# Full-height low queries, an early second normalisation and 14 instead of 12 block products in a hybrid attention block

## The chip, the cores and the metric

The kernel runs on one core of a Trainium2 chip. The core has TensorE (PE; its weight loads are shown apart as PEld), VectorE (DVE), ScalarE (ACT), GpSimd (POOL) and SyncE (SP), which here issues the DMA transfers. Each engine works through its own list of instructions in order. The metric is the time of one execution in microseconds (us), as the median of several runs.

## The reference

One layer on x of 2048 tokens by 1024 columns, float32:

```python
xn = rms_norm(x, norm_gain)
proj = xn @ w_in       # qa ka va ga | qb kb vb gb | iq ik iw | za zb
# branch A: 8 heads of 64, chunks of 64 tokens, own chunk + 8 before, relative bias
ya = chunked_relpos_attention(qa, ka, va, rel_bias) * silu(ga)
# branch B: indexer -> the 256 best keys of each query -> attention on these, one kb/vb for 8 heads
score = sum_h relu(iq_h @ ik.T) * iw_h;  idx = top_k(score, 256)
yb = softmax(qb @ kb[idx].T) @ vb[idx] * silu(gb)
merged = sigmoid(za + b0) * (ya @ w_branch_a) + sigmoid(zb + b1) * (yb @ w_branch_b)
out = rms_norm(x + merged @ w_out, final_norm_gain)
```

## The kernel before, in words

Numbers are kept as pairs: a float32 value is split into a high part (a rounded copy) and a low part (what is left), and a product of two values is three matmuls, high by high, high by low, low by high (`mm3`, L214). A split is a copy by ScalarE and a subtraction by VectorE or GpSimd. Scores of branch A hold both parts of a key's 64 dims on the 128 rows of `kk`; the query's high part stands on both halves (`m = 0`), and its low part on 64 rows alone (`m = 1`), so each score tile is one matmul over 128 rows and one over 64 (L899).

The stages, with their place in the profiled execution:

- To about 119 us: x is loaded and normalised, and the indexer's columns and kb are made.
- 119 to 774 us: the projection. Tokens stand in four groups of 512, and two groups fit into SBUF at a time (slots 0 and 1 of `xh`, `xl`). The columns form 20 units of 256. The list `jobs` first takes all units for groups 0 and 1, then va and some "rest" units for groups 3 and 2. Between them these groups are loaded and normalised into the slots again (`norm_again`, `split_x`: one VectorE instruction scales by gain and root, L226, ScalarE copies, L227, VectorE subtracts, L228); GpSimd makes sums of the blocks on the way (L1214 to L1217), and what others need later goes through scratch memory (`xnD`, `sumD`).
- Beside it runs the search for the 256 best keys: TensorE makes logits (L476), ScalarE takes their positive part (L478), VectorE adds them up (L483) and then brackets a threshold for each query (L511 to L566). `pump` writes search steps into the program while a budget lasts: after each pair of chains `tick` grants `PUMP`, or `PUMP2` in the rest units, times a factor. At the end a check (L574 to L578) asks whether any query has missed its count; TensorE takes part in it with one matmul.
- About 800 to 1050 us: 12 "quads". For groups 3 and 2 a unit is made as a product of two-by-two blocks with 7 products of 12 matmuls in place of 8 (84 for 96); `QUADS` names the units, `prep_full` makes the combinations of weights, `first` and `rest_of` the products.
- About 1050 to 1925 us: the attention. `a_unit` (4 groups by 8 heads, L899 scores, L903 exponentials, L933 transposes, L943 values) and `b_unit` (L1008, L1011, L1025, L1033) interleave by a cost table, with the products with the branch weights (`branch`) between them. A score tile goes from TensorE to VectorE (bias, running minimum, L830), to ScalarE (exponential), back to TensorE (transpose), to ScalarE with VectorE or GpSimd (split, L846 to L854), and to TensorE again.
- To the end: the product with w_out and the last normalisation.

The order on each engine is set by a scheduler that models the time of each instruction as the program is written; `prep`, `tick` and the place in `jobs` decide where something can stand. SP issues nearly all transfers, in its order.

Of the kernel before, what the change touches and what calls it, by code (L numbers as in the profile page):

```python
# [8 lines left out]
F32 = mybir.dt.float32  # L9
# [30 lines left out]
BLOCKS = [2, 4, 5, 6, 7, 8, 9, 10, 11, 12, 13, 14, 15, 3]  # L40
PUMP, PUMP2 = 4500, 6900
SQD = (2,)
# [9 lines left out]
WE = False  # L52
QUADS = "za ka za gb za ka gb qb ga qa ga qa"
WSB, NB = 4, 5
# [25 lines left out]
def f32(ap):  # L80
    return ap.bitcast(F32)
# [11 lines left out]
def block_kernel(ctx: ExitStack, tc: tile.TileContext, io, dbg=None):  # L93
# [11 lines left out]
    def scratch(name, shape, dt=F32):  # L105
        if dbg is not None and name in dbg:
            return nc.dram_tensor("dbg_" + name, shape, dt, kind="ExternalOutput").ap()
        return dram.tile(shape, dt, name=name)
# [14 lines left out]
    sBD = [scratch(f"sBD{g}", [D, 512]) for g in range(NG)]  # L123
    xnD = scratch("xnD", [4, 128, 2, 512])
    sumD = scratch("sumD", [4, 4, 128, 512])
# [622 lines left out]
    mid_st = ExitStack()  # L748
    bres = {}

# [18 lines left out]
    def load_sum(n, k):  # L769

        if n == "s3":
            hi, lo = A21(k)
        else:
            hi, lo = (t[:, k] for t in sums_[n])
        nc.sync.dma_start(f32(lo), sumD[("s3", "s1", "s2", "s4").index(n), k])
        nc.scalar.activation(hi, f32(lo), AF.Copy)
        nc.vector.tensor_tensor(lo, f32(lo), f32(hi), op=OP.subtract)  # L777

# [77 lines left out]
    def load_a(G, h):  # L856
        base = max(0, 4 * G - 4)
        q = ld.tile([128, 2, 512], F32R, name="qs", tag="qs")
        for hl, half in ((0, 0), (0, 1), (1, 0)):
            nc.sync.dma_start(f32(q[half * 64:half * 64 + 64, hl, :]), qA[G][hl, :, h, :])  # L860
        kk = ld.tile([128, 1024], F32R, name="kk", tag="kk")
        v = ld.tile([128, 8, 128], F32R, name="vs", tag="vs")
        for i, g in enumerate(range(max(0, G - 1), G + 1)):
            nc.sync.dma_start(f32(kk[:, i * 512:i * 512 + 512]), kA[g].rearrange("l r h n -> (l r) h n")[:, h, :])
            nc.sync.dma_start(f32(v[:, 4 * i:4 * i + 4]), vA[g][h])
        return base, q, kk, v

    def a_unit(G, h):
        st = {}

        def loads():
            if "ld" not in st:
                st["ld"] = load_a(G, h)
            if h % 2 == 0 and wz is not None:
                sg = wz.tile([128, 512], F32, name="sg", tag="sg", bufs=SGB)
                nc.sync.dma_start(sg, gAD[G][(h // 2) * 128:(h // 2) * 128 + 128])
                shared["sg", "a", h // 2] = sg

        def one():
# [8 lines left out]
            for j in range(4):  # L888
# [6 lines left out]
                for a, w, add in segs:  # L895
                    s_ps = next_s()
                    ko = (f - base) * 128 + a
                    for m, r in ((0, 128), (1, 64)):
                        nc.tensor.matmul(s_ps[:, :w], q[:r, m, j * 128:(j + 1) * 128], kk[:r, ko:ko + w],  # L899
                                         start=(m == 0), stop=(m == 1))  # L900
                    softmax_piece(s_ps[:, :w], add, a == 0, P[:, j, a:a + w], mx[:, j:j + 1])
                    yield
# [286 lines left out]

    rate = [PUMP]  # L1190

    def tick(x):
        if threads:
            pump(rate[0] * x)
        elif not early_:
            close_search()

    again = []

    def norm_again(g):  # L1200

        def part(k):
            xs = tkl.tile([128, 2, 512], F32, name="xs", tag="xs", bufs=2)
            nc.sync.dma_start(xs, io["xT"][g][:, k::4, :])
            if g == 2:
                xa = tkl.tile([128, 2, 512], F32, name="xa", tag="xa", bufs=1)
                nc.sync.dma_start(xa, xnD[k])
            for z in range(2):
                split_x(SLOT[g], k + 4 * z, xs[:, z], roots[g])
            if g == 3:  # L1210
                nc.sync.dma_start(xnD[k], xs)
                return
            e = nc.gpsimd
            e.tensor_tensor(xa[:, 1], xa[:, 1], xa[:, 0], op=OP.add)  # L1214
            e.tensor_tensor(xa[:, 0], xs[:, 0], xa[:, 0], op=OP.subtract)
            e.tensor_tensor(xs[:, 0], xa[:, 1], xs[:, 0], op=OP.subtract)
            e.tensor_tensor(xs[:, 1], xs[:, 1], xs[:, 0], op=OP.subtract)  # L1217
            for t, n in ((xa, 0), (xs, 2)):
                nc.sync.dma_start(sumD[n:n + 2, k].rearrange("s p n -> p s n"), t)

        return [lambda k=k: part(k) for k in range(4)]
# [40 lines left out]
    for i, (how, r_, u, g) in enumerate(jobs):  # L1262
        kind, c2 = UNITS[u]
        wt, s_ = wcur[r_], SLOT[g]
        if r_ >= nu and kind != "va":
            rate[0] = PUMP2
        for c in range(4 if kind == "va" else 2):
            acc = next_acc(i)
            if kind == "va":
# [5 lines left out]
                if again and c % 2 == 0:  # L1275
                    again.pop(0)()
                tick(0.25 if busy else 0.5)
            else:
# [5 lines left out]
                for _ in range(1 if busy and len(again) < 3 else 2):  # L1284
                    if again:
                        again.pop(0)()
                tick(0.5 if busy else 1)
        if (u, g) in ((b_, 0), (b_, 1)) and r_ < nu:
# [216 lines left out]
```

## Time and profile before

| | |
|---|---|
| median of 3 runs | 2142.16 us (2142.09 to 2147.2) |
| profiled execution | 2150.47 us, span 2148.4 us, granted TensorE clock 0.986 |
| TensorE, its weight loads | 2083.8 us (97%), 1713.9 us (80%) |
| VectorE, ScalarE, GpSimd | 68%, 59%, 36% |
| DMA | 327.45 MB, mean 152 GB/s |

A row of a group names line, engine, operation, output and inputs, shape and count; then busy time in us and the mean of one in ns; then idle time of the engine just before them and what ended it. A row of a windows table gives a stretch in us and the busy time of each engine in it, with counts, the granted clock, the share of the DMA engines' time and GB/s. A row of waits names who waited for whom: us in total, times, longest. "128\*128" or "64\*128" ahead of a shape are the rows and columns of the stationary operand.

### The profile page before, as it was taken

To read this page: it belongs to the slowest core of one execution; us is meant where nothing else is said; L and a number is where in the kernel's file an instruction comes from. 1 tells how busy PE (TensorE), PEld (TensorE's weight loads), DVE (VectorE), ACT (ScalarE), POOL (GpSimd) and SP (SyncE) were. 2 spreads that over 40 slices of the span, in tenths; PEclk is the share of its full clock that TensorE was granted. 3 is DMA by queue.
4 is the path that set the end of the run, shared out by engine and by line. 5 is a ranking of instruction groups with operands and counts; after the bars stand their busy time and mean duration, and the time that the engine had idled before them with its cause. 6 is when DMAs were issued, how large, how long until landed. Compare 5 with 4: busy or idle time off the path is not lost.

```text
span 2148.4 us, 33517 instructions
## 1 busy us (share of the span) xinstructions
PE 2083.8 (97%) x10730; PEld 1713.9 (80%) x10730; DVE 1450.5 (68%) x3712; ACT 1273.2 (59%) x2590; POOL 774.5 (36%) x931
## 2 busy tenths in 40 slices
PE   7799999999989999999899999999999999999998
PEld 7688888898878887877677888888878888887886
DVE  6758888869689737555456767756775677865444
ACT  5456675565655625554368768757876688873221
POOL 2131112222153127554235464445334543443420
PEclk9899999999999999999979999999999999999999
DMA  9473333444475325333656563455245531145642
GB/s 357 144 258 119 122 111 118 160 148 142 170 255 170 141 98 179 123 128 120 216 158 199 152 196 114 150 160 169 82 123 165 184 103 52 45 132 190 205 150 88
DMA packets 223044, 327.45 MB, mean 152 GB/s; under 512 B 28304, under 2 KB 99344, under 8 KB 222736
## 3 DMA queue, kind: packets, MB, share of 16 engines
q1 hardware_dynamic: 222864, 325.28, 47.2%
q8 instruction: 85, 1.39, 0.3%
q14 instruction: 95, 0.78, 0.1%
HBM read 215.13 MB, written 110.07 MB: 151 GB/s over the span
## 4 chain that ended last, share of the span: by engine, by line
PE 74%; DMA 11%; DVE 5%; POOL 4%; issue 3%; ACT 2%; SPq 1%; another core or an unknown queue 0%; DVEq 0%; POOLq 0%; ACTq 0%
PE acc L214 27%; PE d L214 8%; PE O L1033 6%; PE po L1400 6%; PE s L899 6%; PE s L1008 6%; PE pt L1025 6%; DMA wst<-wS 4%; PE O L943 4%; PE pt L933 3%; PE lg L476 3%; DMA mf<-mD 1%; POOL wst L1255 1%; DMA xrow<-x 1%; DMA wst<-wP 1%
## 5 line engine op out<-in xcount | busy, mean ns | idle before, releaser
L214 PE MATMUL acc<-xh,wt 128*128 128x512 f32 x1920 | 623.8, 395 | 5.4 <-DVE e L334 2.3
L214 PEld LDWEIGHTS acc<-xh,wt 128*128 128x128 f32 x1920 | 360.3, 188 | 91.6 <-ACT wt L1259 4.6
L214 PE MATMUL acc<-xl,wt 128*128 128x512 f32 x960 | 377.6, 393 | 0.1
L206 POOL TENSOR_TENSOR wt<-wst,wt 128x512 fp32r<-128x512 f32 (+1 forms) x116 | 150.7, 1329 | 471.9 <-ACT wt L205 443.3
L851 POOL TENSOR_TENSOR ptl<-pf,pth 128x512 fp32r<-128x512 f32 (+1 forms) x144 | 179.1, 1244 | 194.8 <-ACT pf L847 148.5
L854 DVE TENSOR_TENSOR ptl<-pt,pth 128x512 fp32r<-128x512 f32 (+1 forms) x288 | 187.3, 660 | 41.6 <-ACT pth L853 40.4
L214 PEld LDWEIGHTS acc<-xl,wt 128*128 128x128 f32 x960 | 181.0, 189 | 40.6 <-DVE xl L777 0.4
L478 ACT ACTIVATE lg<-lg 128x512 f32<-128x512 f32 (+2 forms) x304 | 152.4, 526 | 100.3 <-PE lg L476 97.9
L483 DVE SCALAR_TENSOR_TENSOR sc<-lg,iw,sc 128x512 f32<-128x512 f32 (+2 forms) x266 | 179.5, 679 | 42.0 <-ACT lg L478 37.2
L1008 PE MATMUL s<-kBt,qsB 128*128 128x512 f32 (+3 forms) x640 | 188.6, 386 | 1.1 <-DVE mx L830 0.8
L853 ACT ACTIVATE pth<-pt 128x512 fp32r<-128x512 f32 (+1 forms) x288 | 159.7, 577 | 41.2 <-PE pt L1025 19.2
L899 PE MATMUL s<-kk,qs 128*128 128x256 f32 (+2 forms) x464 | 165.4, 397 | 6.8 <-DVE mx L830 5.4
L1025 PE MATMUL pt<-ident,P 128*128 128x128 f32 x1088 | 165.9, 275 | 0.4 <-DVE ptl L854 0.2
L1011 ACT ACTIVATE P<-P,mx 128x128 f32<-128x128 f32 (+15 forms) x128 | 154.2, 1207 | 19.6 <-DVE mx L830 19.1
L1033 PE MATMUL O<-ptl,vBt 128*128 128x256 f32 x544 | 148.4, 300 | 1.0 <-POOL ptl L851 1.0
L1033 PE MATMUL O<-pth,vBt 128*128 128x256 f32 x544 | 148.0, 292 | 0.3
L830 DVE CUSTOM_DVE_ANT_0 P<-s,mk,mx 128x512 f32<-128x512 f32 (+2 forms) x192 | 125.2, 652 | 30.8 <-PE s L1008 25.3
L1025 PEld LDWEIGHTS pt<-ident,P 128*128 128x128 f32 x1088 | 125.6, 140 | 14.1 <-issue 2.6
L899 PEld LDWEIGHTS s<-kk,qs 128*128 128x128 f32 x464 | 90.2, 194 | 58.3 <-issue 33.0
L1071 POOL TENSOR_TENSOR dw<-dst,dw 128x512 fp32r<-128x512 f32 x64 | 82.6, 1291 | 133.8 <-ACT dw L1070 130.4
L214 PE MATMUL acc<-wt,xh 128*128 128x288 f32 x512 | 106.4, 302 | 12.8 <-DVE sm L547 4.7
L903 ACT ACTIVATE P<-P,mx 128x640 f32<-128x640 f32 (+4 forms) x128 | 97.6, 764 | 34.6 <-DVE mx L830 33.5
(286 smaller groups left out, 4599.5 us busy)
## 6 DMA issues: line engine op xcount, KB each, us to landing
wst<-wP SPq DMA_DIRECT2D x108, 256.0 KB
kk<-kA SPq DMA_DIRECT2D x56, 256.0 KB
vs<-vA SPq DMA_DIRECT2D x56, 256.0 KB
wst<-wS SPq DMA_DIRECT2D x48, 256.0 KB
qs<-qA SPq DMA_DIRECT2D x96, 128.0 KB
xrow<-x SPq DMA_DIRECT2D x16, 512.0 KB
sBD<-ef SPq DMA_DIRECT2D x32, 256.0 KB
vA<-eh SPq DMA_DIRECT2D x32, 256.0 KB
```

What stands on the lines that cost most here:

```text
L206: nc.gpsimd.tensor_tensor(wt[:, 1, k:k + n, c * 128:(c + 1) * 128], st, f32(hi), op=OP.subtract)
L214: nc.tensor.matmul(acc, a, b, start=(first and i == 0), stop=(last and i == n - 1), **({} if first and last else {"skip_group_check": True}))
L478: nc.scalar.activation(lg, lg, AF.Relu)
L483: nc.vector.scalar_tensor_tensor(o_, lg, wv, o_, op0=OP.mult, op1=OP.add)
L851: nc.gpsimd.tensor_tensor(lo, pf, f32(hi), op=OP.subtract)
L853: nc.scalar.activation(hi, src, AF.Copy)
L854: nc.vector.tensor_tensor(lo, src, f32(hi), op=OP.subtract)
L899: nc.tensor.matmul(s_ps[:, :w], q[:r, m, j * 128:(j + 1) * 128], kk[:r, ko:ko + w], start=(m == 0), stop=(m == 1))
L1008: nc.tensor.matmul(s_ps[:, :w], q[:, h, :], kBt[:, m, a:a + w], start=(m == 0), stop=(m == 1))
L1011: nc.scalar.activation(P[:, e, :n], P[:, e, :n], AF.Exp, bias=mx[:, e:e + 1], scale=-1.0, accum_out=st["sum"][:, (u % 2) * 2 + e:(u % 2) * ...
L1025: nc.tensor.transpose(pt[:, k, e, :], P[:, e, (kt + k) * 128:(kt + k + 1) * 128], ident)
L1033: nc.tensor.matmul(o_, vBt[:, kt + k, :], src[:, k, :], start=(kt + k == 0 and n_ == 0), stop=(kt + k == b and n_ == 1), skip_group_check= ...
```

## The change

1. `QUADS` names 14 units: two zb units go from the rest units (which then are 4) to the quads.
2. `norm_early` takes what `norm_again` did on a tile of its own: in jobs 6 to 20 the four parts of group 3 and of group 2 are loaded, scaled by ScalarE (gain) and multiplied by GpSimd (root), and written to scratch memory, each group to its own (`xnD2`, `xnD3`); the sums follow on GpSimd. `norm_again` now loads the finished values into the low half of the slot, and `split_in_place` makes the high half by a ScalarE copy and subtracts it in place on VectorE.
3. `load_a` uses two standing tiles for branch A's queries. Rows 64 to 128 of their low half are set to zero once by GpSimd; both matmuls of a score tile then run over 128 rows.
4. Budgets: `PUMP` is 5300 beside za, zb, ga, gb and 4500 beside qb, va, ka, qa; `PUMP2` 9000 in place of 6900; factors while a new group is being split are 0.35 and 0.75 in place of 0.25 and 0.5.

```diff
-PUMP, PUMP2 = 4500, 6900
+PUMP, PUMP2 = (5300, 4500), 9000
+DVE_KINDS = ("qb", "va", "ka", "qa")
+EN0, TQ = 6, 0.75
...
-QUADS = "za ka za gb za ka gb qb ga qa ga qa"
+QUADS = "za ka za gb za ka gb zb zb qb ga qa ga qa"
...
-    xnD = scratch("xnD", [4, 128, 2, 512])
+    xnD = {g: scratch(f"xnD{g}", [4, 128, 2, 512]) for g in (2, 3)}
...
-        q = ld.tile([128, 2, 512], F32R, name="qs", tag="qs")
+        if len(qz) < 2:
+            qz.append(ld.tile([128, 2, 512], F32R, name=f"qz{len(qz)}", tag="qs"))
+            nc.gpsimd.memset(f32(qz[-1][64:128, 1]), 0.0)
+        q = qz[rot("qz", 2)]
...
-                    for m, r in ((0, 128), (1, 64)):
-                        nc.tensor.matmul(s_ps[:, :w], q[:r, m, j * 128:(j + 1) * 128], kk[:r, ko:ko + w],
+                    for m in range(2):
+                        nc.tensor.matmul(s_ps[:, :w], q[:, m, j * 128:(j + 1) * 128], kk[:, ko:ko + w],
                                          start=(m == 0), stop=(m == 1))
...
+    def norm_early(g, k):
+
+        xs = tkl.tile([128, 2, 512], F32, name="xs", tag="xs", bufs=2)
+        nc.sync.dma_start(xs, io["xT"][g][:, k::4, :])
+        if g == 2:
+            xa = tkl.tile([128, 2, 512], F32, name="xa", tag="xa", bufs=1)
+            nc.sync.dma_start(xa, xnD[3][k])
+        e = nc.gpsimd
+        for z in range(2):
+            nc.scalar.activation(xs[:, z], xs[:, z], AF.Copy, scale=gcol[:, k + 4 * z:k + 4 * z + 1])
+            e.tensor_tensor(xs[:, z], xs[:, z], roots[g], op=OP.mult)
+        nc.sync.dma_start(xnD[g][k], xs)
+        if g == 3:
+            return
+        e.tensor_tensor(xa[:, 1], xa[:, 1], xa[:, 0], op=OP.add)
...
+    def split_in_place(hi, lo):
+
+        nc.scalar.activation(hi, f32(lo), AF.Copy)
+        nc.vector.tensor_tensor(lo, f32(lo), f32(hi), op=OP.subtract)
+
     def norm_again(g):
 
         def part(k):
-            xs = tkl.tile([128, 2, 512], F32, name="xs", tag="xs", bufs=2)
-            nc.sync.dma_start(xs, io["xT"][g][:, k::4, :])
...
             for z in range(2):
-                split_x(SLOT[g], k + 4 * z, xs[:, z], roots[g])
...
+                hi, lo = block(SLOT[g], z)(k)
+                nc.sync.dma_start(f32(lo), xnD[g][k][:, z])
+                split_in_place(hi, lo)
...
-        if r_ >= nu and kind != "va":
-            rate[0] = PUMP2
+        rate[0] = PUMP[kind in DVE_KINDS] if r_ < nu or kind == "va" else PUMP2
+        if EN0 <= i < EN0 + 16 and i % 2 == 0:
+            norm_early(3 - (i - EN0) // 8, (i - EN0) // 2 % 4)
...
-                tick(0.25 if busy else 0.5)
+                tick(0.35 if busy else 0.5)
...
-                tick(0.5 if busy else 1)
+                tick(TQ if busy else 1)
```

Three places show how the order moves. The first is VectorE's order where a group is made anew beside the search. `xs` holds loaded tokens, `xh`/`xl` the halves of a slot, `sc`/`lg` the search's scores and logits. Before:

```order
L483 SCALAR_TENSOR_TENSOR sc<-lg,iw,sc 128x384
L226 SCALAR_TENSOR_TENSOR xs<-xs,gcol,roots_135 128x512 x2
L483 SCALAR_TENSOR_TENSOR sc<-lg,iw,sc 128x384
L226 SCALAR_TENSOR_TENSOR xs<-xs,gcol,roots_135 128x512 x2
L228 TENSOR_TENSOR xl_122<-xs,xh_121 128x512
L483 SCALAR_TENSOR_TENSOR sc<-lg,iw,sc 128x384
L228 TENSOR_TENSOR xl_124<-xs,xh_123 128x512
```

and in the changed program, for the parts of group 2 in slot 0:

```order
L1230 TENSOR_TENSOR xl_119<-xl_119,xh_118 128x512
L568 TENSOR_SCALAR far<-sc 128x1792
L555 TENSOR_SCALAR jk,over<-sc,st 128x1920
L485 SCALAR_TENSOR_TENSOR sc<-lg,iw,sc 128x512 x2
L1230 TENSOR_TENSOR xl_119<-xl_119,xh_118 128x512
L711 SCALAR_TENSOR_TENSOR el<-acc,eh 128x512
L558 SCALAR_TENSOR_TENSOR sc<-jk,sc 128x1920
```

The scaling is gone from VectorE there; what is left is the subtraction, in place, between logits and search steps. The second place is GpSimd's order in the first half of the projection. `wt` are weights that it splits, `xa` the tile for the sums. Before:

```order
L1214 TENSOR_TENSOR xa<-xa 128x512
L206 TENSOR_TENSOR wt<-wst,wt 128x4x128 x44
L196 TENSOR_TENSOR wt<-wst,wt 128x8x32
L206 TENSOR_TENSOR wt<-wst,wt 128x4x128 x4
L196 TENSOR_TENSOR wt<-wst,wt 128x8x32
L206 TENSOR_TENSOR wt<-wst,wt 128x4x128 x20
L1215 TENSOR_TENSOR xa<-xs,xa 128x512
```

and changed:

```order
L208 TENSOR_TENSOR wt<-wst,wt 128x4x128 x4
L1216 TENSOR_TENSOR xs<-xs,roots_135 128x512 x4
L1221 TENSOR_TENSOR xa<-xs,xa 128x512
L1222 TENSOR_TENSOR xs<-xa,xs 128x512
L1223 TENSOR_TENSOR xs<-xs 128x512
L1220 TENSOR_TENSOR xa<-xa 128x512
L1221 TENSOR_TENSOR xa<-xs,xa 128x512
L1222 TENSOR_TENSOR xs<-xa,xs 128x512
L208 TENSOR_TENSOR wt<-wst,wt 128x4x128 x2
```

The multiplications by the root (L1216) are new there, and the sums follow them at once, where before some seventy weight splits stood between the first sum and the next. The third place is SP's order around the reload. `wst` are weights on their way in, `qA` stores of the unit qa, `mskD` the masks that the search has finished. Before:

```order
L1204 DMA xs<-xT 128x2x512 x2
L712 DMA qA_61<-eh 128x512
L712 DMA qA_61<-el 128x512
L1211 DMA xnD<-xs 128x1024
L453 DMA iqT<-iqD 32x8x128 x3
L1211 DMA xnD<-xs 128x1024
L453 DMA iqT<-iqD 32x8x128
L712 DMA qA_60<-eh 128x512
L1204 DMA xs<-xT 128x2x512 x2
```

and changed:

```order
L205 DMA wst<-wP 128x512 x2
L1237 DMA xl_119<-xnD_98 128x512
L714 DMA qA_60<-eh 128x512
L205 DMA wst<-wP 128x512
L714 DMA qA_60<-el 128x512
L1237 DMA xl_119<-xnD_98 128x512 x2
L1237 DMA xl_121<-xnD_98 128x512
L1237 DMA xl_119<-xnD_98 128x512
L1237 DMA xl_121<-xnD_98 128x512 x3
L569 DMA mskD<-far 128x1792
```

The loads of x and the stores of normalised values are no longer there; the reloads go straight into the low half of the slot, behind the stores of the unit that used the slot last.

More of the change, by code (lines that the diff above doesn't have):

```diff
@@ L748, in block_kernel @@
     mid_st = ExitStack()
-    bres = {}
+    bres, qz = {}, []
     def close_search():
@@ L775, in load_sum @@
         nc.sync.dma_start(f32(lo), sumD[("s3", "s1", "s2", "s4").index(n), k])
-        nc.scalar.activation(hi, f32(lo), AF.Copy)
-        nc.vector.tensor_tensor(lo, f32(lo), f32(hi), op=OP.subtract)
+        split_in_place(hi, lo)
     def open_early():
@@ L857, in load_a @@
         base = max(0, 4 * G - 4)
-        q = ld.tile([128, 2, 512], F32R, name="qs", tag="qs")
+        if len(qz) < 2:
+            qz.append(ld.tile([128, 2, 512], F32R, name=f"qz{len(qz)}", tag="qs"))
+            nc.gpsimd.memset(f32(qz[-1][64:128, 1]), 0.0)
+        q = qz[rot("qz", 2)]
         for hl, half in ((0, 0), (0, 1), (1, 0)):
-            nc.sync.dma_start(f32(q[half * 64:half * 64 + 64, hl, :]), qA[G][hl, :, h, :])
+            nc.sync.dma_start(f32(q[half * 64:half * 64 + 64, hl]), qA[G][hl, :, h, :])
         kk = ld.tile([128, 1024], F32R, name="kk", tag="kk")
@@ L873, in loads @@
                 st["ld"] = load_a(G, h)
-            if h % 2 == 0 and wz is not None:
+            if wz is None:
+                return
+            if h % 2 == 0:
                 sg = wz.tile([128, 512], F32, name="sg", tag="sg", bufs=SGB)
@@ L1188, in attention @@
                 early(early_w[i])
-    rate = [PUMP]
+    rate = [PUMP[0]]
     def tick(x):
@@ L1198, in block_kernel @@
     again = []
+    def norm_early(g, k):
[10 more added lines that the diff above has]
+        if g == 3:
+            return
+        e.tensor_tensor(xa[:, 1], xa[:, 1], xa[:, 0], op=OP.add)
+        e.tensor_tensor(xa[:, 0], xs[:, 0], xa[:, 0], op=OP.subtract)
+        e.tensor_tensor(xs[:, 0], xa[:, 1], xs[:, 0], op=OP.subtract)
+        e.tensor_tensor(xs[:, 1], xs[:, 1], xs[:, 0], op=OP.subtract)
+        for t, n in ((xa, 0), (xs, 2)):
+            nc.sync.dma_start(sumD[n:n + 2, k].rearrange("s p n -> p s n"), t)
+    def split_in_place(hi, lo):
+        nc.scalar.activation(hi, f32(lo), AF.Copy)
+        nc.vector.tensor_tensor(lo, f32(lo), f32(hi), op=OP.subtract)
     def norm_again(g):
         def part(k):
-            xs = tkl.tile([128, 2, 512], F32, name="xs", tag="xs", bufs=2)
-            nc.sync.dma_start(xs, io["xT"][g][:, k::4, :])
-            if g == 2:
-                xa = tkl.tile([128, 2, 512], F32, name="xa", tag="xa", bufs=1)
-                nc.sync.dma_start(xa, xnD[k])
-            for z in range(2):
-                split_x(SLOT[g], k + 4 * z, xs[:, z], roots[g])
[L1210 to L1219, printed above, removed]
+            for z in range(2):
+                hi, lo = block(SLOT[g], z)(k)
+                nc.sync.dma_start(f32(lo), xnD[g][k][:, z])
+                split_in_place(hi, lo)
         return [lambda k=k: part(k) for k in range(4)]
```

## The prediction

> **What bounds the kernel now.** I read the page first, then the windows table by stage, then the waits of TensorE in the stretches that the change touches, and last the rows of single operations by shape. The page says which engine carries the whole:
>
> ```profile
> span 2148.4 us, 33517 instructions
> PE 2083.8 (97%) x10730; PEld 1713.9 (80%) x10730; DVE 1450.5 (68%) x3712; ACT 1273.2 (59%) x2590; POOL 774.5 (36%) x931
> PE 74%; DMA 11%; DVE 5%; POOL 4%; issue 3%; ACT 2%; SPq 1%; another core or an unknown queue 0%; DVEq 0%; POOLq 0%; ACTq 0%
> ```
>
> TensorE is busy for 97% of the span and holds 74% of the chain that ended last. So only three things shorten this kernel: fewer matmuls, cheaper matmuls, or less of the remaining 65 us of TensorE idleness. The windows (us; busy time of PE, PEld, DVE, ACT, POOL with counts; clock; DMA share; GB/s) show where the other engines come close:
>
> ```profile
> 119.00:774.00 655.00, 642.13 (x3112) 540.91 (x3111) 531.22 (x1315) 386.98 (x733) 163.86 (x124) 0.99 0.48 156
> 600.00:675.00 75.00, 62.13 (x391) 57.09 (x390) 72.59 (x161) 40.70 (x83) 38.32 (x29) 0.95 0.68 220
> 774.00:797.00 23.00, 23.00 (x102) 18.39 (x101) 0.18 (x2) 5.48 (x9) 5.10 (x4) 1.00 0.14 52
> 845.00:1050.00 205.00, 200.95 (x858) 159.82 (x857) 116.61 (x268) 99.46 (x258) 95.07 (x190) 1.00 0.38 125
> 1275.00:1375.00 100.00, 99.60 (x621) 81.65 (x620) 78.63 (x222) 85.43 (x178) 46.70 (x48) 1.00 0.40 118
> 1475.00:1600.00 125.00, 124.19 (x779) 101.60 (x778) 96.71 (x270) 103.33 (x199) 51.13 (x53) 1.00 0.33 99
> 1725.00:1850.00 125.00, 124.34 (x792) 103.71 (x791) 98.01 (x271) 102.45 (x183) 45.81 (x44) 1.00 0.20 61
> 1125.00:1875.00 750.00, 745.78 (x4474) 615.66 (x4473) 527.15 (x1454) 563.44 (x1119) 345.17 (x334) 1.00 0.45 136
> ```
>
> In the projection with the search beside it (119 to 774) VectorE is busy for 81%. Between 600 and 675, where groups 3 and 2 are normalised again, it is busy for 97% and TensorE stands still for 12.9 us. From 774 to 797 VectorE has nothing left while TensorE works on until it reaches the check: the search is 23 us early. In the attention TensorE is over 99% busy.
>
> **The two moved units.** Two ordinary units leave the stage with the search: 192 matmuls of 512 columns. They come back as two quads of 84, so 168. A matmul's price is read from an undisturbed piece of the chain:
>
> ```profile
> 721.18 69.55 PE acc L214 x300
> ```
>
> 69.55/300 = 0.2318 us. Minus 192 x 0.2318 = 44.5, plus 168 x 0.2318 = 38.9: -5.6. The quads have some waits of their own: 205 - 200.95 = 4.05 us in the 858/84 = 10.2 quads of that window, 0.4 each, so +0.8. Sum -4.8 us. The quads' other work (weight combinations on GpSimd, splits on ScalarE and VectorE) lies under TensorE at 46 to 57% of those engines.
>
> **The normalisation made early.** What it takes from VectorE are 16 instructions of the first row; the subtractions stay:
>
> ```profile
> L226 DVE SCALAR_TENSOR_TENSOR xs<-xs,gcol,roots 128x512 f32<-128x512 f32 x16 | 14.7, 957 | 7.9 <-DMA xs<-xT 7.9
> ```
>
> So VectorE's work beside the projection falls from 531.2 to 516.5 us. ScalarE's 16 new scalings, at the 0.63 us of its copies of that size, are 10 us on an engine that is 59% busy there (386.98/655):
>
> ```profile
> L227 ACT ACTIVATE xh<-xs x16: 611/632/656, 577.7 to 646.2; 128x512 fp32r<-128x512 f32 x16
> ```
>
> For GpSimd's 16 multiplications a piece of the timeline gives a price, and what they can cost VectorE:
>
> ```profile
> 666.30 0.17 DVE L538 TENSOR_SCALAR msk<-st 128x2 int32<-128x2 f32 x1
> ...
> 666.76 2.56 POOL L206 TENSOR_TENSOR wt<-wst,wt 128x512 fp32r<-128x512 f32 x2 [10.64 <-ACT wt L205]
> 666.78 1.30 DVE L544 TENSOR_TENSOR sm<-st 128x4 f32<-128x4 f32 x1
> ```
>
> Two operations of this size take GpSimd 2.56 us, so 1.28 each and 21 us for 16, on an engine that is 25% busy (163.86/655). But a tiny operation of VectorE takes 1.30 us beside them and 0.17 without. In the worst case 16 x 1.3 = 21 us of VectorE's time are lost, more than the 14.7 saved; in the best nothing. The rows show a blocked and a free case side by side, so I take half, 10 us: a net gain of about 4.
>
> The Trainium skill (SBUF — State Buffer, Who interferes with whom) says that a VectorE instruction with two inputs in SBUF and a GpSimd instruction that reads SBUF shut each other out of a shared port, the later one for the whole of the other. It speaks against the change, and the rows above bear it out. By it each of the 16 can hold VectorE for its whole length: the worst case above, with which VectorE needs 516.5 + 21 = 537 us, and the sum would lose its -6.
>
> What do the waits of TensorE between 600 and 675 make of it?
>
> ```profile
> PE acc L214 <- DVE sm L547: 4.7, 1, 4.7
> PE acc L214 <- DVE el L709: 3.4, 2, 2.0
> PE acc L214 <- DVE vv L717: 3.4, 1, 3.4
> PE acc L214 <- DVE eh L723: 1.2, 2, 0.6
> ```
>
> All of them end on a VectorE that is late. Part of the 16 multiplications stand in this stretch (the rows below show their tile loaded at 638), with their sums, loads and stores; all of that is now far ahead of it. In their place stand 16 reloads of 256 KB into the low halves. Each waits for TensorE's last read of the old group; behind it on SP's queue stand the stores of qA, the next weight loads and a mask store, and behind the subtraction on VectorE the next logits, for which ScalarE and TensorE wait. A store and a load of 512 KB near this place took:
>
> ```profile
> 630.96 7.08 DMA sumD<-xs
> 638.05 4.63 DMA xs<-xT
> ```
>
> So a reload that VectorE meets too early costs several us. Bounds: -12.9 (every wait goes) and +13 (as much again). I take -6, nearer to the gain, because the VectorE work there becomes less.
>
> The four more table loads of ScalarE and the memsets of the standing tiles fall into the quads (ScalarE 49%, GpSimd 46% busy) and cost nothing there; without that cover they are 4 x 1.28:
>
> ```profile
> 1071.52 1.28 ACT L903 ACT_TABLE_LOAD   x1 [1.49 <-DVE mx L830]
> ```
>
> **The low queries on 128 rows.** For branch A's scores each pair of matmuls now has one of 128 rows and one of 64. Branch B's pairs (L1008) have the same widths and 128 rows in both. By shape (count, busy us, mean ns):
>
> ```profile
> L899 PE MATMUL s<-kk,qs 64*128 64x384 f32 x112 | 50.9, 455 | 0.0
> L899 PE MATMUL s<-kk,qs 128*128 128x384 f32 x112 | 45.2, 403 | 5.4 <-DVE mx L830 5.4
> L1008 PE MATMUL s<-kBt,qsB 128*128 128x384 f32 x112 | 31.2, 362 | 0.3 <-DVE mx L830 0.3
> ...
> L899 PE MATMUL s<-kk,qs 64*128 64x256 f32 x104 | 40.2, 387 | 0.0
> L899 PE MATMUL s<-kk,qs 128*128 128x256 f32 x104 | 36.1, 347 | 0.2
> L1008 PE MATMUL s<-kBt,qsB 128*128 128x256 f32 x112 | 24.9, 307 | 0.4 <-DVE mx L830 0.2
> ...
> L899 PE MATMUL s<-kk,qs 64*128 64x128 f32 x16 | 6.2, 389 | 0.0
> L899 PE MATMUL s<-kk,qs 128*128 128x128 f32 x16 | 5.6, 349 | 1.2 <-DVE ptl L854 1.2
> L1008 PE MATMUL s<-kBt,qsB 128*128 128x128 f32 x16 | 2.8, 288 | 0.0
> ```
>
> A pair of 384 costs (50.9 + 45.2)/112 = 0.858 us of busy time in branch A and 2 x 31.2/112 = 0.557 in branch B: 0.301 more, for half the rows in one of the two. For 256 it is 0.734 against 0.445, 0.289 more; for 128 0.738 against 0.35, 0.39 more. In all 112 x 0.301 + 104 x 0.289 + 16 x 0.39 = 70 us, 0.302 for each of 232 pairs. The extra stands on both members of a pair, so I read it as a price of passing between 64 and 128 rows, which the change does away with.
>
> How much of the 70 us arrives at the end? That depends on what stands close behind TensorE. Branch A's matmuls of the stretches in which ScalarE is fullest, and of the whole attention:
>
> ```profile
> 1275.00:1375.00 100.00, 24.88 (x72) 13.37 (x72) 1.00 0.40 118
> 1475.00:1600.00 125.00, 27.91 (x81) 14.91 (x80) 1.00 0.33 99
> 1725.00:1850.00 125.00, 23.30 (x66) 12.27 (x66) 1.00 0.20 61
> 1125.00:1875.00 750.00, 133.29 (x384) 71.36 (x384) 1.00 0.45 136
> ```
>
> The three full stretches hold 219 matmuls, 110 pairs, 33 us of the extra. ScalarE is busy there for 291.2 of 350 us, 83%; if all 33 went, it would be 92%. Waits for exponentials and splits must then appear, and I take three quarters, 25 us. The other 82 pairs (24.8 us) lie where ScalarE is at (563.4 - 291.2)/400 = 68%: nine tenths, 22 us. The remaining 40 pairs lie before 1125, in the beginning of the attention, where TensorE waits for others (the 5.4 us in the second row of shapes): a third of 12, 4 us. Together -51; bounds -21 (nothing in the full stretches, 17 and 4 beside them) and -70.
>
> **The sum** on the profiled execution of 2150.5 us (span 2148.4): -4.8 - 6 - 51 = -62, 2088.5. That execution is 8.3 us longer than the median of the three runs, and I carry the difference, not the time: 2142.2 - 62 = 2080 us.
>
> **The search's end** is the cover under all this. TensorE now reaches the check at 797 - 44.5 - 6 = 746.5. VectorE's 516.5 us at the old share of 81% end at 119 + 637 = 756, 9.5 us late, which would make 2090. The larger budgets (5300 instead of 4500 beside the gate units) write the search earlier into VectorE's order, so that it finds work in the 124 us in which it is idle now; to be in time it needs 516.5/627.5 = 82%. I expect that and count nothing, but let my own range reach there.
>
> **Rivals.** *ScalarE becomes the bound of the attention:* only 21 of the 70 arrive, 2142 - 32 = 2110. For it speaks the 83 to 85%; against it that TensorE waited for hardly anything in that stage (4.2 us of idleness in 750).
>
> *Everything arrives:* 70 + 13 + 5, 2054 us. Against it the same 83%.
>
> *The rows don't matter:* no gain in the scores, 2142 - 11 = 2131. The Trainium skill (TensorE: Matmul & The Clock Gate, Why this matters for your kernels) says that a single matmul with K=32 takes the same time as one with K=128; by that alone the edit would be worth nothing. Another of its pages (TensorEngine Tiling (Array Packing), Key Properties) says that a change of tiling mode drains TensorE. Only a price of the change explains why the 128-row member is dear too (403 ns against 362), so I give this rival little.
>
> *Slower: VectorE stands before the reloads.* Its 16 subtractions sit in order between logits and search steps. Should each wait for its load as long as the load in the two rows above, 4.63 us, VectorE loses 74 us, the search ends at 756 + 74 = 830, and TensorE waits at the check for 83 us: 2080 + 83 = 2163. The 62 us of gain are gone once VectorE's loss passes 62 - 9.5 = 52 us, 3.3 us for each subtraction. Against it: before the 16 multiplications VectorE was idle for 7.9 us in all, half a microsecond each, although these waited for loads too. For it: the loads wait for TensorE now.
>
> **Chances and range.** My forecast 0.70 (2062 to 2104, which takes in a check that is up to 24 us late); ScalarE as the bound 0.13; everything arrives 0.06; rows don't matter 0.04; waits at the reloads 0.07, of which 0.04 past the point where the kernel is slower and 0.03 close to it, with no change to be seen. A measurement of this kernel tells about 0.3% (6.4 us) from no change. That makes faster 0.93, same 0.03, slower 0.04. The range 2050 to 2118 takes in the forecast, most of the case in which everything arrives and most of ScalarE as the bound, and leaves under 2 in 10 outside.
>
> **What would show it.** In the changed kernel's groups by shape: no row of 64 x 384 for L899's successor, and both members of its pairs at 0.28 us of busy time or less for 384 columns; if they stay at 0.4, the third term is wrong. In the windows: ScalarE at 88 to 92% in the full stretches of the attention with few waits of TensorE on ScalarE; long ones make the first rival right. Between the start of the reloads and the check: TensorE's idleness below 12.9 us, VectorE at 83% or more, and VectorE's idle time before the in-place subtractions below 10 us; if TensorE stands at the check for over 25 us, the cover is gone and the time leaves my range. The quads should last 2 x 84 x 0.2318 + 0.8 = 40 us longer than before.

## The result, and the profile after

The changed kernel takes 2092.45 us (median; 2089.03 to 2094.56, 4 runs), the kernel before 2144.68 us beside it. The ratio is 0.9749, with a 95% interval of 0.9717 to 0.9781. The profiled execution has a span of 2087.2 us, 61.2 us shorter than before. This pair of executions flatters the change: by the medians the gain is 52 us, and the interval allows 47 to 61. The page of the changed kernel, span, busy time and the chain of waits by engine:

```profile
span 2087.2 us, 33654 instructions
PE 1997.9 (96%) x10706; PEld 1693.9 (81%) x10706; DVE 1475.8 (71%) x3746; ACT 1285.5 (62%) x2644; POOL 809.9 (39%) x981
PE 53%; DMA 4%; DVE 2%; ACT 2%; issue 1%; POOL 1%; SPq 1%; DVEq 0%; ACTq 0%; POOLq 0%
```

The chain is followed back only so far that its shares add up to 64%, so its 53% for TensorE cannot be set against the 74% of before. TensorE lost 86 us of busy time (modelled, since the profile computes the end of a matmul) with only 24 matmuls fewer. The groups by shape say where (the same columns as before; L905 is branch A's scores, L1014 branch B's):

```profile
L905 PE MATMUL s<-kk,qz 128*128 128x384 f32 x224 | 65.5, 374 | 6.4 <-DVE mx L831 6.3
L905 PE MATMUL s<-kk,qz 128*128 128x256 f32 x208 | 47.0, 307 | 1.2 <-DVE mx L831 0.9
L1014 PE MATMUL s<-kBt,qsB 128*128 128x384 f32 x112 | 31.5, 363 | 0.3 <-DVE mx L831 0.2
```

There is no 64-row shape any more, and a member of branch A's pairs costs 65.5/224 = 0.29 us of busy time for 384 columns, just above the 0.28 named as the sign, where branch B's cost 31.5/112 = 0.28. The start of branch A's scores to the start of the final product was 858.7 us (1057.5 to 1916.2) and is 795.5 us (1060.4 to 1855.9). That is 63 us less. But 24 matmuls of the last quad moved from behind the first scores to ahead of them; at 0.2318 us each, 5.6 us left the attention and entered the quads. Without this shift the attention gave 58 us, and all that lies ahead of it together became 3 us shorter, though it was to become 11 us shorter.

The windows show the reason. First before, then after, for the beginning of the projection:

```profile
118.00:250.00 132.00, 132.00 (x587) 108.40 (x586) 100.64 (x322) 84.28 (x178) 31.97 (x25) 1.00 0.48 161
```

```profile
118.00:250.00 132.00, 123.02 (x531) 96.16 (x530) 104.10 (x259) 84.02 (x179) 71.47 (x56) 1.00 0.73 247
```

TensorE, never idle there before, now stands for 9 us. It also does 56 matmuls fewer in the window (531 for 587), which is 13 us at 0.2318 us each, so its idle time understates what it lost. GpSimd has twice the work (71.5 for 32.0 us). VectorE is busy for 3.5 us more with 63 instructions fewer. The waits of TensorE in the changed kernel, from 118 to 250 and from 560 to 700, and at the start of the attention:

```profile
PE lg L478 <- DVE sc L485: 8.6, 8, 2.0
...
PE lg L478 <- DVE sc L485: 7.3, 3, 3.7
...
PE s L905 <- DMA kk<-kA: 7.8, 3, 4.8
```

Logits wait for an accumulator that VectorE (L485) has not read yet. What keeps VectorE can be read from its timeline, just ahead of one of these waits:

```profile
156.03 3.82 POOL L208 TENSOR_TENSOR wt<-wst,wt 128x512 fp32r<-128x512 f32 x3
156.13 1.22 DVE L522 TENSOR_TENSOR sm<-sm 128x2 f32<-128x2 f32 x1
...
157.38 1.22 DVE L523 TENSOR_TENSOR sm<-sm 128x2 f32<-128x2 f32 x1
...
158.64 1.24 DVE L524 TENSOR_SCALAR sm<-sm 128x2 f32<-128x2 f32 x1
...
159.91 0.16 DVE L525 TENSOR_TENSOR sm<-sm 128x2 f32<-128x2 f32 x1
...
162.04 0.89 PE L478 MATMUL lg<-ikT,iqT 128*128 128x512 f32 x2 [1.65 <-DVE sc L485]
```

Three operations on 128 x 2 elements take 1.2 us each, one for each operation of GpSimd, and 0.16 when it is done. Between 118 and 250, 6 operations that read and write at most 16 elements a row took over 0.45 us before, and 29 do now; beyond 0.16 us each they lose 5.6 us and 26.4 us. (The expectations below count 8 and 31, with two that write 8 elements but read whole rows.) Not every short operation is held: the 49 reciprocals of 128 x 2 stay at 0.16 us (mean 162 ns before, 159 now).

### The profile page after: what moved, and what is told of

It is laid out like the page before. It is cut to its first block, busy times and chain, and to the rows that moved or that the text cites. A ratio compares the mean times of both kernels' runs of the same rounds, so it can differ in the third digit from the quotient of the medians.

```text
span 2087.2 us, 33654 instructions
## 1 busy us (share of the span) xinstructions
PE 1997.9 (96%) x10706; PEld 1693.9 (81%) x10706; DVE 1475.8 (71%) x3746; ACT 1285.5 (62%) x2644; POOL 809.9 (39%) x981
## 3 DMA queue, kind: packets, MB, share of 16 engines
q1 hardware_dynamic: 225744, 331.57, 49.2%
## 4 chain that ended last, share of the span: by engine, by line
PE 53%; DMA 4%; DVE 2%; ACT 2%; issue 1%; POOL 1%; SPq 1%; DVEq 0%; ACTq 0%; POOLq 0%
PE acc L216 12%; PE po L1420 9%; PE d L216 8%; PE O L1039 6%; PE s L1014 5%; PE pt L1031 5%; PE O L949 3%; PE s L905 3%; PE pt L939 3%; DMA dst<-wA 1%; DMA kk<-kA 1%; DMA dst<-wB 1%; DVE P L831 1%; DMA ost<-wO 1%; DVE ptl L855 0%
## 5 line engine op out<-in xcount | busy, mean ns | idle before, releaser
L216 PE MATMUL acc<-xh,wt 128*128 128x512 f32 x1856 | 599.3, 394 | 5.7 <-DVE e L336 2.4
L216 PEld LDWEIGHTS acc<-xh,wt 128*128 128x128 f32 x1856 | 347.2, 188 | 84.4 <-DVE e L336 2.6
L216 PE MATMUL acc<-xl,wt 128*128 128x512 f32 x928 | 363.8, 393 | 0.0
L208 POOL TENSOR_TENSOR wt<-wst,wt 128x512 fp32r<-128x512 f32 (+1 forms) x108 | 145.4, 1375 | 419.8 <-ACT wt L207 303.4
L216 PEld LDWEIGHTS acc<-xl,wt 128*128 128x128 f32 x928 | 174.5, 188 | 38.7
L485 DVE SCALAR_TENSOR_TENSOR sc<-lg,iw,sc 128x512 f32<-128x512 f32 (+2 forms) x266 | 178.6, 678 | 26.1 <-ACT lg L480 21.9
L1014 PE MATMUL s<-kBt,qsB 128*128 128x512 f32 (+3 forms) x640 | 188.0, 385 | 1.3 <-DVE mx L831 0.9
L480 ACT ACTIVATE lg<-lg 128x512 f32<-128x512 f32 (+2 forms) x304 | 147.9, 521 | 44.5 <-PE lg L478 43.6
L478 PE MATMUL lg<-ikT,iqT 128*128 128x512 f32 (+2 forms) x304 | 111.3, 378 | 18.0 <-DVE sc L485 17.9
L905 PE MATMUL s<-kk,qz 128*128 128x256 f32 (+2 forms) x464 | 113.8, 341 | 15.4 <-DMA kk<-kA 7.8
L533 ACT ACTIVATE jk<-sc,st 128x640 int8<-128x640 f32 (+6 forms) x49 | 71.2, 1453 | 84.3 <-DVE st L551 73.6
L1014 PEld LDWEIGHTS s<-kBt,qsB 128*128 128x128 f32 x640 | 102.9, 190 | 15.8 <-DVE mx L831 9.1
```

The costliest lines, as they stand in the source:

```text
L216: nc.tensor.matmul(acc, a, b, start=(first and i == 0), stop=(last and i == n - 1), **({} if first and last else {"skip_group_check": True}))
L480: nc.scalar.activation(lg, lg, AF.Relu)
L485: nc.vector.scalar_tensor_tensor(o_, lg, wv, o_, op0=OP.mult, op1=OP.add)
L905: nc.tensor.matmul(s_ps[:, :w], q[:, m, j * 128:(j + 1) * 128], kk[:, ko:ko + w], start=(m == 0), stop=(m == 1))
L1014: nc.tensor.matmul(s_ps[:, :w], q[:, h, :], kBt[:, m, a:a + w], start=(m == 0), stop=(m == 1))
```

## Experiments

In the edits the names are those of the diff. "Alone" means on top of the kernel before.

### Low queries on 128 rows, alone

The third part of the diff, put into the kernel before.

> The kernel before with the third part of the change alone: standing query tiles with a zero half, low queries on 128 rows. Theory (passing between 64 and 128 rows costs 0.3 us a pair): the pairs fall to about 0.56 us for 384 columns, the attention from 859 to about 800 us, the whole 52 to 63 us faster than before. Rival (rows do not matter, the gain of the changed kernel arose elsewhere): within 10 us of before. Rival (ScalarE bounds the attention): 20 to 35 us faster.

Measured: 2083.07 us beside 2148.82, ratio 0.9709 (0.9688 to 0.9731). That is the whole gain of the change; whether it is more, the overlapping intervals do not tell. The attention takes 795.9 us (858.7 before) with the same matmuls in the same order. TensorE's busy time in it falls by 78 us, from 846.5 to 768.9, and its idle time rises from 12.2 to 26.9 us. The weight loads of branch A's scores stood still for 33.0 us in 153 gaps before, for which the profile names no other engine, and do so for 5.1 us in 2 gaps now. Ahead of the attention little has changed, as the waits of TensorE in the search stage show:

```profile
PE acc L214 <- DVE sm L547: 4.8, 1, 4.8
PE acc L214 <- DVE vv L717: 3.2, 1, 3.2
PE acc L214 <- DVE el L709: 2.8, 2, 2.0
```

The gain is a little more than my 52 to 63, so both rivals fall.

### The other parts without it

```diff
-                    for m in range(2):
-                        nc.tensor.matmul(s_ps[:, :w], q[:, m, j * 128:(j + 1) * 128], kk[:, ko:ko + w],
+                    for m, r in ((0, 128), (1, 64)):
+                        nc.tensor.matmul(s_ps[:, :w], q[:r, m, j * 128:(j + 1) * 128], kk[:r, ko:ko + w],
```

> The changed kernel with the low queries' matmuls on 64 rows again (the standing tiles stay); all other parts as changed. Theory: the attention goes back to about 850 us and the whole to 2092 + 57 = 2149, so that the other three parts together are worth nothing or cost up to 8 us. Rival (the other parts carry a share of the gain, as my sum of -11 says): 2130 to 2138.

Measured: 2148.98 us beside 2148.82, ratio 1.0008 (0.9994 to 1.0022). The attention takes 854.5 us again, as the theory has it. The other three parts together are worth nothing that can be measured.

### What rows cost by themselves

> None of the reference is computed, zeros are written. Only runs of matmuls of 384 columns with changing stationary operands: 200 over 128 rows, 200 over 64, 200 alternating, 208 in blocks of eight of one kind, 200 in the order 128, 64, 64, 128. Theory (the price is for passing): about 0.176 us each for 128 rows and for 64 rows, about 0.32 to 0.33 each when alternating (0.15 for each pass), 0.19 to 0.20 in blocks of eight, 0.25 in the order 128, 64, 64, 128. Rival (64 rows are slow in themselves): 64 rows cost 0.3 or more each and blocks of eight cost the mean of the two kinds. Rival (rows never matter): all five alike.

The windows of the probe's sections, in order: 128 rows, 64 rows, alternating, blocks of eight, the order 128, 64, 64, 128, and 128 rows once more (length, busy TensorE with its count, weight loads, the other engines; the last three numbers are the granted clock, the share of the DMA engines and GB/s):

```profile
101.00:135.00 34.00, 34.00 (x198) 34.00 (x197) 0.00 (x0) 0.00 (x0) 0.00 (x0) 1.00 0.00 1
136.00:170.00 34.00, 34.00 (x198) 34.00 (x197) 0.00 (x0) 0.00 (x0) 0.00 (x0) 1.00 0.00 0
171.00:291.00 120.00, 120.00 (x198) 55.73 (x198) 0.00 (x0) 0.00 (x0) 0.00 (x0) 0.51 0.00 0
292.00:335.00 43.00, 43.00 (x209) 36.38 (x208) 0.00 (x0) 0.00 (x0) 0.00 (x0) 0.95 0.00 0
335.00:389.00 54.00, 54.00 (x199) 29.18 (x197) 0.00 (x0) 0.00 (x0) 0.00 (x0) 1.00 0.00 1
390.00:424.00 34.00, 34.00 (x198) 34.00 (x197) 0.00 (x0) 0.00 (x0) 0.00 (x0) 1.00 0.00 0
```

128 rows and 64 rows alike take 34/198 = 0.172 us. Alternating takes 120/198 = 0.61 us where 0.32 to 0.33 was expected, at a granted clock of 0.51; if all of it goes with the clock, that is 0.31 at the full clock (an estimate). Blocks of eight take 43/209 = 0.206, but their first 4 us still ran at half clock; from 300 us on they take 0.198, which is 8 x (0.198 - 0.172) = 0.21 us for each pass from one kind to the other. The order 128, 64, 64, 128 takes 54/199 = 0.271, and 2 x (0.271 - 0.172) = 0.20 us for each pass. The 0.15 that I expected was too little for the probe. In the kernel the 78 us of busy time that the 128-row run saved in the attention, over 464 passes, are 0.17 each. So rows by themselves cost nothing here and the pass does: both rivals fall.

Ahead of a pass the weight load starts 0.25 us after the load before it has ended; in a uniform section the loads follow one another (busy for 34.00 of 34 us, but 29.18 of 54 in the order 128, 64, 64, 128). The trace agrees with the Trainium skill's rule that K=32 takes the time of K=128 (TensorE: Matmul & The Clock Gate, Why this matters for your kernels), as far as 64 rows tell: 0.172 us for both. The pass also fits the drain at a change of tiling mode of which the Trainium skill tells (TensorEngine Tiling (Array Packing), Key Properties); that it is this drain, no run shows. My rival read the first rule without the second.

### The multiplication on VectorE

```diff
-            nc.scalar.activation(xs[:, z], xs[:, z], AF.Copy, scale=gcol[:, k + 4 * z:k + 4 * z + 1])
-            e.tensor_tensor(xs[:, z], xs[:, z], roots[g], op=OP.mult)
+            nc.vector.scalar_tensor_tensor(xs[:, z], xs[:, z], gcol[:, k + 4 * z:k + 4 * z + 1], roots[g],
+                                           op0=OP.mult, op1=OP.mult)
```

> The changed kernel with the early scaling as one VectorE instruction for gain and root, in place of a ScalarE scaling and a GpSimd multiplication; 16 instructions of about 0.75 us come to VectorE (12 us), 16 of 1.28 leave GpSimd. Theory (GpSimd's reads hold up VectorE's short operations: 31 of over 0.45 us between 118 and 250, 27 us in excess, against 8 and 7 before): the number of long short ones there falls to 10 to 15, TensorE's waits for L485 from 8.6 to below 5 us, the whole 2 to 6 us faster than the changed kernel. Rival (VectorE just has too much to do in that stretch): the waits grow to 10 to 15 us and the whole is 2 to 6 us slower.

Measured: 2094.24 us, ratio 0.9752 (0.9728 to 0.9777), not to be told from the changed kernel. The window from 118 to 250:

```profile
118.00:250.00 132.00, 122.39 (x527) 97.15 (x526) 110.08 (x272) 74.42 (x162) 52.38 (x40) 0.99 0.75 247
```

TensorE is idle for 9.6 us. The short operations of over 0.45 us fall only from 29 to 23 (31 to 25 by the count of the expectation), since the sums and weight splits on GpSimd stay; what VectorE regains (6 us) is less than the 13.0 us of the 16 instructions that it now does itself. Both expectations named a part of it, neither the balance.

### The budgets of before

```diff
-PUMP, PUMP2 = (5300, 4500), 9000
+PUMP, PUMP2 = (4500, 4500), 6900
```

with the factors 0.25 and 0.5 of before.

> The changed kernel with the budgets and factors of before (4500, 6900, 0.25, 0.5). Theory one (the early normalisation makes VectorE late between 118 and 250): TensorE still stands there for 7 to 10 us. Theory two (the larger budgets ask VectorE for more search work than it can do there): the early idleness falls below 3 us. By both the search now is written later; if its end passes TensorE's arrival at the check (about 746), TensorE stands there and the whole is 5 to 25 us slower than the changed kernel; otherwise it is within 8 us of it.

Measured: 2097.68 us, ratio 0.9775 (0.9755 to 0.9795); the interval overlaps that of the changed kernel, so the 5 us more are not certain. The early wait stays, so it isn't from the budgets, and a new one comes behind the check (waits from 118 to 250, and from 770 to 820):

```profile
PE lg L478 <- DVE sc L485: 7.8, 7, 2.3
...
PE acc L216 <- ACT wv L1278: 11.1, 3, 9.9
```

That wait is not for the search but for the first quad's weights: three of its seven weight matrices are made only after the search has closed, so a search that is written to the end of the stage leaves no time for them. Here the first of them is begun 18 us after the check, and from the check to the first product with them TensorE has 28 matmuls to do, 6 us at 0.2318 each. In the changed kernel they are begun after 16 us, and TensorE has 146 matmuls, 34 us, to do until then; it does not wait for them.

### The early parts spread, without and with a hold

In every third job instead of every second (6 to 27):

> The changed kernel with its eight early parts of the normalisation in every third job from 6 to 27, in place of every second from 6 to 20. Theory one (GpSimd's dense work beside VectorE's short operations): the early idleness of 9.0 us falls to 3 to 6 us, some of it appears after 250, the whole is 2 to 6 us faster than the changed kernel. Theory two (the budgets): no difference in it, within 2 us.

Measured: 2090.03 us, ratio 0.9734 (0.9715 to 0.9753); TensorE waits for 9.2 us before 250, as in the changed kernel. This does not tell the theories apart: GpSimd's multiplications stand at 129 to 208 us in its timeline, though the last belong to job 27, which starts at about 455 us: the scheduler drew them all ahead. With a hold they cannot be:

```diff
-    def norm_early(g, k):
+    def norm_early(g, k, gate):
...
+        nc.gpsimd.tensor_copy(xs[:, 0, 0:1], gate)
         nc.sync.dma_start(xs, io["xT"][g][:, k::4, :])
...
-        if EN0 <= i < EN0 + 16 and i % 2 == 0:
-            norm_early(3 - (i - EN0) // 8, (i - EN0) // 2 % 4)
+        if EN0 <= i < EN0 + 24 and (i - EN0) % 3 == 0:
+            norm_early(3 - (i - EN0) // 12, (i - EN0) // 3 % 4, f32(wt[:, 1, KT - 1, 255:256]))
```

`gate` is one element of the job's split weights.

> The changed kernel with each early part held until the weights of its job are split (a copy of one element into its tile), in every third job from 6 to 27: unlike in the spread run, the parts cannot be drawn ahead, and GpSimd's multiplications and sums lie at most one part to 35 us. Theory (GpSimd's dense work costs VectorE its time there): TensorE's idleness before 250 falls from 9.0 to below 3 us, VectorE's excess in long short operations to below 70 us, the whole 4 to 8 us faster than the changed kernel. Rival (VectorE is late for another reason, as the order of the logits): 7 us and more stay.

Measured: 2088.13 us, ratio 0.9749 (0.9728 to 0.977). The early idleness went from 9.0 to 0.1 us, as the theory has it, and the time did not move: TensorE's idleness from 118 us to the check is 19.6 us, for 18.3. It waits for the same operation later, from 250 on. The loss in short operations moved with it rather than going away: up to the check it is 58.4 us, for 63.9 in the changed kernel and 59.5 in the spread run without a hold (76.0 for 81.5 by the count of the expectation, which had below 70), but from 250 on it is 49.2 us, for 37.6 in the changed kernel. Waits of this run from 118 to 600:

```profile
PE lg L478 <- DVE sc L485: 9.8, 11, 3.1
```

### Parts two and one, each with 128 rows alone

> The kernel with 128-row low queries and the early normalisation, but with 12 quads and the budgets of before: against the run with 128-row queries alone (2083) it shows the second part by itself. Theory one: TensorE is idle for 5 to 9 us before 250 and for 5 us less than 11.8 between 560 and 700; 2083 to 2090. Theory two (the early waits come from the budgets): nothing early, 5 us less late; 2076 to 2080.

Measured: 2090.59 us, ratio 0.9742 (0.9724 to 0.9761), where 128 rows alone had 0.9709. That is 7 us more, with intervals that just overlap. The window of this run, and TensorE's waits in it:

```profile
118.00:250.00 132.00, 122.77 (x522) 96.29 (x522) 101.62 (x254) 81.57 (x171) 69.33 (x55) 0.99 0.71 242
```

```profile
PE lg L478 <- DVE sc L485: 9.1, 8, 2.0
```

So the early normalisation by itself brings the 9 us; between 560 and 700 TensorE is idle for 6.5 us, for 11.8.

> The kernel with 128-row low queries and 14 quads, but the normalisation and the budgets of before: the first part without what makes room for it. The search then still ends at about 774, and TensorE reaches the check at 795 - 50 = 745. Theory (the search's end is the cover): TensorE stands at the check for 20 to 30 us, the whole 2083 - 5 + 25 = 2098 to 2108. Rival (the scheduler fits the search into the shorter stage by itself): no wait of over 5 us at the check, 2076 to 2084.

Measured: 2097.22 us, ratio 0.9762 (0.974 to 0.9785). Two more quads alone cost 11 us by the ratios, 14 by the profiled spans (2081.6 and 2095.3). TensorE is idle for 13 us more up to the attention (52.3 for 39.3 us); the 24 matmuls saved (6 us) and an attention some 5 us longer (see the end) about cancel. The wait (770 to 820) is again that for the weights, and not for the search, as I had it:

```profile
PE acc L214 <- ACT wv L1262: 11.2, 3, 9.9
```

The first of them is begun 18 us after the check, and TensorE has 26 matmuls to do until then. With 128 rows alone there are 107, 25 us, and the wait is 0.4 us. Neither expectation had this.

### The held parts with 12 and 13 quads

The hold above, 128 rows, and the budgets of before:

> 128-row low queries and the early normalisation held in the same way, with 12 quads and the budgets of before. Theory: against the run without the holding (2090.6) the early 9.2 us go, the 5 us saved between 560 and 700 stay: 2080 to 2084, 0 to 3 us better than 128-row queries alone (2083). Rival: 2087 or more.

Measured: 2075.57 us beside 2142.60, ratio 0.9688 (0.9666 to 0.9709). This beats both kernels: the interval lies below that of the changed kernel (0.9717 to 0.9781). Against 128 rows alone (0.9688 to 0.9731) the intervals overlap. The same window now:

```profile
118.00:250.00 132.00, 132.00 (x588) 108.41 (x587) 96.80 (x317) 88.12 (x184) 39.98 (x34) 1.00 0.51 172
```

VectorE does 317 instructions in 96.8 us, where 254 took it 101.6 without the hold, and TensorE is never idle. It does 588 matmuls for 522, 15 us more at 0.2318 each, about what the whole run gains over that without the hold (12 us by the ratios, 15 by the spans) and more than the theory had. VectorE's loss in short operations up to the check is 40.8 us, for 53.9 without the hold and 37.3 with 128 rows alone.

> As the last, with 13 quads: one unit of zb leaves the stage with the search. TensorE reaches the check some 22 us earlier, about when the search ends. Theory (the search has 20 us to spare, one unit fits, two do not): 12 matmuls fewer, 0 to 3 us faster than the last, with no wait of over 5 us near the check. Rival (the first quad's weights come late once the search ends close to the check): 3 to 8 us slower.

Measured: 2084.95 us, ratio 0.9726 (0.9709 to 0.9743), some 9 us more for one unit moved; the rival holds. The first quad's weights are begun 19 us after the check, and TensorE has 50 matmuls, 12 us, to do until it needs them. Waits from 780 to 830:

```profile
PE acc L216 <- ACT wv L1279: 12.1, 3, 10.8
```

### The larger budgets with 12 quads

> The held early parts and the larger budgets (5300, 9000) with 12 quads: between the held run of the changed kernel (2088.1, idle 19.6 us up to the check) and that of 12 quads with the old budgets (2075.6, idle 9.9). Theory (the larger budgets ask VectorE for logits and search faster than it can do them, and TensorE waits at the logits): 8 us and more of idleness at the logits between 250 and 560, 2082 to 2088. Rival (the shorter stage, so the 14 quads, makes VectorE late): idleness as with the old budgets, 2073 to 2078.

Measured: 2088.98 us, ratio 0.9754 (0.9739 to 0.9769), against 0.9688 with the old budgets. Waits from 118 to 600, first with the old budgets, then with the larger ones:

```profile
PE lg L478 <- DVE sc L483: 2.1, 1, 2.1
PE lg L478 <- DVE sc L485: 1.1, 2, 0.8
```

```profile
PE lg L478 <- DVE sc L485: 9.0, 11, 3.1
PE lg L478 <- DVE sc L483: 0.8, 2, 0.6
PE lg L478 <- DVE st L539: 0.5, 2, 0.3
```

With the larger budgets TensorE waits 7 us longer at the logits, with 12 quads as with 14: the rival falls. Two things come together here that no run separates: VectorE is asked for more at a time, and its short operations lose 58.3 us up to the check, for 40.8. Of the 14 us between the two profiled spans (2072.9 and 2087.2) 8 lie ahead of the attention, 6 of these idleness of TensorE. Another 6 lie in the attention (793 and 799 us), where the two run the same code, though the scheduler put its matmuls in another order (739 of 4941 places differ); I have not found what they are.

## Why the prediction was right, and where not

**The bound.** TensorE sets the end, and the cheaper matmuls are the gain: right. 2080 was forecast, 2092 measured, inside the range. The sum says -62, the medians say -52 (47 to 61 by the interval). That the profiled spans say -61.2 is luck: the profiled execution of the changed kernel was the shortest of its four (2089.03), and that of before (2150.47) was longer than the median. And behind the sum stand two errors of opposite sign.

**The low queries: -51 forecast, -63 measured with this part alone.** The cause (the pass, not the rows) was right: the probe and the run alone show it. Both sizes in the term were too small. The price was 70 us, read from branch B's pairs; TensorE's busy time in the attention fell by 78 us, 65 of them in the rows of the pairs (184.2 to 119.0 us) and the rest in other matmuls. And more of it arrived: 63 of 78 us, 81%, where I had 51 of 70, 73%, with three quarters in the full stretches and a third at the beginning. ScalarE did come to 89% and 86% in such stretches of the changed kernel:

```profile
1265.00:1365.00 100.00, 98.79 (x666) 87.51 (x665) 80.56 (x228) 88.92 (x183) 47.22 (x48) 1.00 0.48 145
1455.00:1575.00 120.00, 117.06 (x809) 104.19 (x807) 96.74 (x269) 103.54 (x200) 51.77 (x51) 1.00 0.36 113
```

but TensorE was idle there for only 1.2 and 2.5% of the time. At the beginning, from the first score of branch A to the first of branch B, the same 225 matmuls took 66.7 us and take 56.0 with 128 rows alone: TensorE's busy time fell by 17 us and its idle time rose by 6, so 11 of 17 us arrived, for the 4 of 12 that I took.

**The normalisation made early: -6 forecast, +5 measured** (TensorE's idleness from 118 us to the check, 18.3 for 12.9 us). This is the step that failed. Between 600 and 700 TensorE's idleness fell from 12.9 to 7.3 us, as forecast. First before, then after:

```profile
600.00:700.00 100.00, 87.13 (x518) 78.52 (x517) 97.46 (x200) 50.44 (x103) 45.28 (x33) 0.97 0.66 208
```

```profile
600.00:700.00 100.00, 92.72 (x553) 84.15 (x552) 86.42 (x183) 60.84 (x124) 25.12 (x18) 0.97 0.54 171
```

But I had spread GpSimd's interference over the stage and taken half of 21 us; VectorE's short operations lost 27 us more than before (63.9 for 36.6 up to the check), 21 of them between 118 and 250, where the scheduler put all the early parts. VectorE was busy for 538 us up to the check, not 516.5:

```profile
119.00:754.00 635.00, 616.73 (x2988) 515.68 (x2987) 538.07 (x1300) 383.18 (x740) 182.44 (x136) 0.99 0.50 166
```

The worst case in my text, 537 us of VectorE and the -6 lost, was the right one. The Trainium skill's rule on the shared port (SBUF — State Buffer, Who interferes with whom) had said so. The trace agrees: 1.22 us for a two-input operation beside GpSimd, 0.16 after it. An operation with one input was held too (L524, 1.24 us), which the rule as I quoted it, for two inputs, does not cover. The runs with the parts held bear the cause out: with 12 quads and the old budgets the early wait of 9.2 us goes to 0.0 and the whole gains 12 to 15 us. With the larger budgets the hold only moves the loss.

**The moved units: -4.8 forecast.** The 24 matmuls went, but the two units are not free to move. Alone they cost 11 to 14 us, because the first quad's weights wait for the search to close; the larger budgets close it earlier (the search ends at 734, the check stands at 753.7), and pay with waits at the logits. I had the cover as the search's end against TensorE's arrival; it was the search's end against the preparation behind it: in the changed kernel and in the runs with such a wait the first of these weights is begun 16 to 19 us after the check, and TensorE waits where it has less than that left to do (26, 28 and 50 matmuls, 6 to 12 us; hardly with 107, and not with 146).

**The rivals.** ScalarE did not become the bound: TensorE's waits that end on it come to 9 us in the whole attention of the changed kernel. VectorE did not stand before the reloads:

```profile
L1230 DVE TENSOR_TENSOR xl<-xl,xh 128x512 fp32r<-128x512 f32 x16 | 11.2, 726 | 0.0
```

It was idle for 0.0 us ahead of its 16 subtractions. "Everything arrives" was nearest for the attention alone.

**Left open.** Why the attention lasts some 5 us longer in all runs with 14 quads or the larger budgets (744 to 746 us from branch B's first score on) than in those with 12 and the old ones (738 to 740; 741 with 13), all with 128 rows. Most of it is idleness of TensorE there (16 to 19 us, for 12 to 14). The order of TensorE's matmuls does not explain it alone: the changed kernel with the budgets of before and the run with 13 quads have the same order there and differ by 4 us. The 7.8 us at its start, for the load of kk, were not tried by themselves.

## What to carry to other kernels

Look at the number of rows from one matmul to the next: in the probe 64 and 128 rows took the same 0.172 us, so padding a short operand with zeros cost nothing here, and saved some 0.2 us at each pass. When an operation moves to GpSimd to relieve VectorE, price it by what VectorE's short operations lose beside it, in the very stretch in which the scheduler will put it, and hold it with a real dependence where a scheduler orders the program, since the place in the program alone did not hold it here. Undo each part of a combined change: here one part gave everything, and the other three together nothing that could be measured.

## Not expected of the hardware

Alternating 128 and 64 rows without other work between brought the granted clock to 0.51 (third row of the probe, one execution), while 64 rows alone, 128 alone and the order 128, 64, 64, 128 ran at 1.00. In the attention before, with transposes and other products between the pairs, the clock stood at 1.00 from 1125 to 1875 us all the same, so the drop goes with the dense alternation of the probe; what in it lowers the clock was not tried.
